# Scratch transposes issued from GpSimd's queue instead of SyncE's, with shorter pauses, in a two-layer decoder trunk

## The chip, the cores and the metric

The kernel runs on one core of a Trainium2 chip. The metric is the device time of one execution in microseconds. A core has five engines that run side by side, each working through its own queue of instructions in order: TensorE (PE; PEld is its weight load), VectorE (DVE), ScalarE (ACT), GpSimd (POOL) and SyncE (SP). They meet at semaphores. Transfers are begun by an instruction in one engine's queue and are then carried by 16 DMA engines.

## The reference, cut to what matters

Two layers over 256 positions of width 2048, each a token mixer and a dense SwiGLU FFN (hidden width 5632). Layer 0 mixes with stick-breaking attention, layer 1 with a gated DeltaNet.

```python
def swiglu(h, w_gu, w_down):
    gate, up = jnp.split(h @ w_gu, 2, axis=-1)
    return (jax.nn.silu(gate) * up) @ w_down

for i in range(DEPTH):
    h = rms_norm(x, mix_norm[i])
    y = stick_breaking_mixer(...) if i == 0 else gated_deltanet_mixer(...)
    x = x + y
    x = x + swiglu(rms_norm(x, ffn_norm[i]), ffn_w_gu[i], ffn_w_down[i])
```

In the attention mixer q and k are normed per head and then multiplied, `z = q k^T`, so both are needed with the head's 128 columns on the partitions. The FFN's product `silu(gate) * up` is needed with its hidden columns on the partitions for the product with `w_down`. Both come out of TensorE the other way round, with the positions on the partitions. They have to be transposed.

## The kernel before

**Products.** All weights are streamed from HBM in pieces (a unit: two tiles of 128 rows by 512 columns, 512 KB). Each operand, weight or activation, is split into a high part in the fast format and a low part with the rest, and three products (high-high, high-low, low-high) give the float32 result. ScalarE makes the high part of a weight piece (`convert`, by `act`, line 328), VectorE the low part (`tt`, line 332), and TensorE multiplies (`mm`, line 354). A stretch of both FFNs runs six pairs of blocks by a scheme with seven products in place of eight (`seven`); its sums of weights are more work for VectorE. Two or three pieces are converted ahead of TensorE.

**Transposes through scratch.** In 36 places a transpose is done without TensorE: VectorE transposes 32 x 32 squares in place (`nc.vector.transpose`, lines 897 and 939), four transfers write the rows to a DRAM scratch tile (`way`), and two transfers read it back in another order. Here this is called a turn, its transfers the writes and the reads. A write moves 32 partitions of 32 x 32 floats in pieces of 128 bytes (128 KB), a read 128 partitions of 4 x 128 floats in pieces of 512 bytes (256 KB). `turn` (from line 891) does it for q and k of the four head groups (8 turns) and for parts of the input of three norms (`TURNED`, 6 turns). `turned_pairs` (from line 933) does it for the FFN's 22 hidden blocks, and then splits the result into high (`kh`) and low (`kl`) parts by `operands_of`. For q a scaling by `qgain` on ScalarE follows, for k nothing: TensorE reads it as it is. At the norms ScalarE and VectorE make `hTh` and `hTl` from it.

**Queues.** All transfers, weights (`load`, line 519) and turns (`dma`, line 367), are begun by SyncE. A read waits for the writes of its turn.

**What sets the order.** The program is written out while a planner keeps a clock for each engine (`self.t`). Work around the products is in tasks, generators that yield where they would wait. At each small step of the products `tick` resumes those tasks whose planned time (`task.ready`) has come, and what a task then issues goes into the engines' queues at that place. So the planned durations decide where in ScalarE's and VectorE's queues the split stands, between the weight conversions. A wrong one does no harm to the result, since semaphores hold the real order, but an instruction that stands too early holds up the queue behind it. For a transfer begun by SyncE the planner counts 0.46 of SyncE's clock, 1.55 to begin, the bytes at a rate, and 0.55 to land. `WAY` is a pause between the transposes and the first write in `turned_pairs` (`TURN` in `turn`), `NAP` the one between its transfers (`STEP` in `turn`): they keep SyncE's queue free for weight loads between the writes.

Of the kernel before, what the change touches and what calls it, by code (L numbers as in the profile page):

```python
# [15 lines left out]
P = 128  # L16
D = 2048
S = 256
NT = S // P
# [12 lines left out]
class Slots:  # L32
# [37 lines left out]
    def put(self, *items):  # L70
        self.free.extend(items)
# [86 lines left out]
class Trunk:  # L158
# [20 lines left out]
    CONST = 14.0  # L179
    EARLY = 6  # L180
    LATER = 1.5
    WAY, NAP = 3.0, 1.2
    TURN, STEP = 1.0, 1.2
    TURNED = ((1, 0), (1, 1), (2, 0), (2, 1), (3, 0), (3, 1))
    GDN_ORDER = [('qk', 0), ('ba',), ('v', 0), ('qk', 1), ('z', 0), ('v', 2), ('v', 1), ('z', 1), ('qk', 2), ('qk', 3), ('v', 3), ('z', 2), ('z', 3), ('out', 0, 4), ('out', 4, 8), ('qk', 4), ('v', 4), ('qk', 5), ('v', 5), ('z', 5), ('z', 4), ('qk', 7), ('v', 6), ('qk', 6), ('out', 8, 16), ('v', 7), ('z', 6), ('z', 7), ('out', 16, 24), ('out', 24, 32)]

# [179 lines left out]
    def dma(self, out, in_):  # L366
        self.nc.sync.dma_start(out, in_)
        n = 4
        for d in out.shape:
            n *= d  # L370
        self.cur.ends("dma", self.transfer(n * (2 if out.shape[-1] * 4 <= 512 else 1), self.cur.begins("dma")))

    def transfer(self, nbytes, ready):
        issue = max(self.t["sp"], ready, self.t["pe"])
        self.t["sp"] = issue + 0.46
        self.t["dma"] = max(self.t["dma"], issue + 1.55) + nbytes / 3.6e5
        return self.t["dma"] + 0.55
# [513 lines left out]
    def turn(self, parts, back=False, src=None):  # L891

        way = yield from self.ways.get()
        for i, s in enumerate(parts):
            self.nc.vector.transpose(s, src[i] if src else s)
            self.spend("dve", 0.07 + 0.00104 * NB)
            self.weave()
        self.cur.later = self.TURN  # L900
        yield
        flat = way[:]
        both = parts[0].tensor is parts[1].tensor and parts[1].offset - parts[0].offset == NB
        apart = not back and not both

        rows = (flat.rearrange("(c t) j -> c (t j)", t=2) if apart else flat).rearrange("(b i) j -> i b j", i=32)
        k = 0
        for a in range(4):
            m = slice(32 * a, 32 * a + 32)
            for n in range(1 if both else 2):  # L910
                if both:
                    dst, at = rows[:, :, m], self.joined(parts[0], 2)[m, :]
                elif back:
                    dst, at = rows[:, 16 * n:16 * n + 16, m], parts[n][m, :]
                else:
                    dst, at = rows[:, :, n * P + 32 * a:n * P + 32 * a + 32], parts[n][m, :]
                self.dma(dst, at.rearrange("p (b j) -> p b j", j=32))
                k += 1
            self.cur.nap = self.STEP if a < 3 else None
            yield  # L920
        for n in range(2):
            if back:
                self.dma(parts[n].rearrange("p (k c) -> p k c", k=4), flat.rearrange("(k t p) c -> t p k c", t=NT, p=P)[n])
            elif apart:
                self.dma(parts[n].rearrange("p (k c) -> p k c", k=2),
                         flat.rearrange("(c t) j -> c (t j)", t=2)[S * n:S * n + S, :].rearrange("(k p) c -> p k c", p=P))
            else:
                self.dma(self.joined(parts[0], 2).rearrange("p (k s) -> p k s", k=4)[:, :, n * P:(n + 1) * P],
                         flat[n * NB:(n + 1) * NB, :].rearrange("(k p) s -> p k s", p=P))
        yield  # L930
        self.ways.put(way)

    def turned_pairs(self, tok, stage, ops, put):

        way = yield from self.ways.get()
        for s, t in zip(self.cut(stage, NB), self.cut(tok, NB)):
            self.nc.vector.transpose(s, t)  # L939
            self.spend("dve", 0.07 + 0.00104 * NB)  # L940
            self.weave()
        self.cur.later = self.WAY
        yield

        rows = way[:].rearrange("(b i) j -> i b j", i=32)
        for a in range(4):
            m = slice(32 * a, 32 * a + 32)
            self.dma(rows[:, :, m], stage[m, :].rearrange("p (b j) -> p b j", j=32))
            self.cur.nap = self.NAP if a < 3 else None
            yield  # L950
        for t in range(NT):
            self.dma(tok.rearrange("p (k s) -> p k s", k=4)[:, :, t * P:(t + 1) * P],
                     way[t * NB:(t + 1) * NB, :].rearrange("(k p) s -> p k s", p=P))
            self.cur.nap = self.NAP if t < NT - 1 else None
            yield
        self.ways.put(way)
        if stage is not tok:
            self.duos.put(stage)
        for n, l in enumerate(self.cut(tok, NB)):
            pair = yield from self.pairs.get()  # L960
            self.operands_of(ops[2 * n:2 * n + 2], pair, l.rearrange("p (k s) -> p k s", k=2))
        put()


    def ffn_units(self, layer, norm, nxt, last, before, ahead=0):
# [52 lines left out]
        for b, n in zip(mids, turn):  # L1018
            b.sets = (n,)
# [773 lines left out]
```

## Time and profile before

| | before |
|---|---|
| time, median of 3 runs | 2709.56 us (2708.41 to 2709.73) |
| profiled execution | 2705.98 us |
| its span on the core | 2704.3 us |
| granted TensorE clock | 1.00 |
| mean DMA rate over the span | 198 GB/s |

The page lists the busy time of each engine, the chain of work that ended last, the waits and the transfers. In a row of the waits, the instruction that waited stands left of the arrow and what it waited for right of it, then the total in us, the number of times and the longest. In a row of the timeline the first two numbers are the start (us from the span's start) and the duration; brackets hold the idle time before it and what ended that. In the view by stretches, the columns after the two lengths are the busy time (with the number of instructions) of PE, PEld, DVE, ACT and POOL, then the granted clock, the DMA engines' busy share and GB/s. In the table of a tile, a row of transfers has the shortest, median and longest time that the begin took in its queue (ns), then the first and last start.

### The profile page before, as it was taken

To read this page: it belongs to the slowest core of one execution; us is meant where nothing else is said; L and a number is where in the kernel's file an instruction comes from. 1 tells how busy PE (TensorE), PEld (TensorE's weight loads), DVE (VectorE), ACT (ScalarE), POOL (GpSimd) and SP (SyncE) were. 2 spreads that over 40 slices of the span, in tenths; PEclk is the share of its full clock that TensorE was granted. 3 is DMA by queue.
4 is the path that set the end of the run, shared out by engine and by line. 5 is a ranking of instruction groups with operands and counts; after the bars stand their busy time and mean duration, and the time that the engine had idled before them with its cause. 6 is when DMAs were issued, how large, how long until landed. Compare 5 with 4: busy or idle time off the path is not lost.

```text
span 2704.3 us, 39527 instructions
## 1 busy us (share of the span) xinstructions
PE 2669.4 (99%) x14730; PEld 2274.6 (84%) x14730; DVE 2182.7 (81%) x3451; ACT 1491.8 (55%) x1961; POOL 11.2 (0%) x95
## 2 busy tenths in 40 slices
PE   9999999999999999999999999999999999999999
PEld 7888888888888888888888888888878888888887
DVE  6556568899999897678778887887679899989885
ACT  6555556554555554565665556645575555555453
POOL 0000000000000000000000000000000000000000
PEclk9999999999999999999999999999999999999999
DMA  7766775787676777855656556556567767767776
GB/s 245 202 185 196 219 211 164 208 231 212 203 218 205 208 211 233 227 174 172 182 143 195 159 161 175 168 153 186 170 191 212 223 196 220 217 188 218 226 209 188
DMA packets 487611, 534.41 MB, mean 198 GB/s; under 512 B 188087, under 2 KB 267258, under 8 KB 487418
## 3 DMA queue, kind: packets, MB, share of 16 engines
q1 hardware_dynamic: 487370, 531.87, 67.1%
q8 instruction: 115, 1.88, 0.3%
q14 instruction: 78, 0.64, 0.1%
q10 hardware_dynamic: 48, 0.02, 0.0%
HBM read 508.20 MB, written 23.59 MB: 197 GB/s over the span
## 4 chain that ended last, share of the span: by engine, by line
PE 83%; DVE 10%; issue 2%; ACT 2%; DMA 2%; SPq 0%; ACTq 0%; DVEq 0%
PE acc L354 61%; PE bank L354 20%; DVE w L332 5%; DVE slabs L332 2%; PE bank L363 1%; DMA slab<-in_ffn_w_gu_dram 1%; ACT slabs L328 1%; ACT w L328 1%; DVE slab L338 1%; DVE slab L332 1%; DVE slab L939 1%; DMA slab<-in_ffn_w_down_dram 0%; ACT slab L328 0%; DVE x L332 0%; DMA w<-in_ffn_w_gu_dram 0%
## 5 line engine op out<-in xcount | busy, mean ns | idle before, releaser
L332 DVE TENSOR_TENSOR w<-w,w 128x1024 fp32r<-128x1024 f32 (+2 forms) x746 | 946.3, 1285 | 249.0 <-ACT w L328 247.6
L328 ACT ACTIVATE w<-w 128x1024 fp32r<-128x1024 f32 (+2 forms) x650 | 802.8, 1244 | 417.8 <-PE acc L354 347.0
L354 PE MATMUL acc<-w,hTh 128*128 128x512 f32 (+1 forms) x3232 | 925.0, 369 | 9.1 <-DVE w L332 8.4
L354 PEld LDWEIGHTS acc<-w,hTh 128*128 128x128 f32 x3232 | 585.9, 189 | 120.5 <-DVE w L332 14.5
L354 PE MATMUL acc<-w,hTl 128*128 128x512 f32 (+1 forms) x1616 | 590.2, 365 | 3.1 <-DVE hTl L338 3.1
L328 ACT ACTIVATE slabs<-slab 128x1024 fp32r<-128x1024 f32 x264 | 279.3, 1058 | 431.9 <-DMA slab<-in_ffn_w_gu_dram 123.8
L332 DVE TENSOR_TENSOR slabs<-slab,slabs 128x1024 fp32r<-128x1024 f32 x264 | 321.5, 1218 | 93.1 <-ACT slabs L328 93.1
L354 PE MATMUL acc<-w,kh 128*128 128x512 f32 x1184 | 369.6, 393 | 0.0
L354 PEld LDWEIGHTS acc<-w,hTl 128*128 128x128 f32 x1616 | 304.5, 188 | 53.5 <-DVE hTl L338 3.9
L332 DVE TENSOR_TENSOR w<-w 128x256 f32<-128x256 f32 (+1 forms) x576 | 291.2, 508 | 9.8 <-DMA w<-in_ffn_w_gu_dram 2.6
L354 PEld LDWEIGHTS acc<-w,kh 128*128 128x128 f32 x1184 | 218.8, 188 | 43.7
L354 PE MATMUL acc<-w,kl 128*128 128x512 f32 x592 | 230.7, 390 | 0.0
L354 PE MATMUL acc<-slabs,hTh 128*128 128x512 f32 x608 | 190.1, 392 | 2.8 <-DVE slabs L332 2.8
L354 PE MATMUL bank<-w,wide 128*128 128x256 f32 x1296 | 178.9, 283 | 0.0
L354 PEld LDWEIGHTS bank<-w,wide 128*128 128x128 f32 x1296 | 165.8, 192 | 0.0
L354 PE MATMUL bank<-slabs,hTh 128*128 128x512 f32 x512 | 159.9, 392 | 3.1 <-DVE slabs L332 3.1
L354 PE MATMUL bank<-slabs,kh 128*128 128x512 f32 x512 | 159.6, 392 | 3.4 <-DVE slabs L332 3.4
L354 PE MATMUL acc<-slabs,kh 128*128 128x512 f32 x480 | 149.9, 392 | 2.1 <-DVE slabs L332 1.9
L354 PEld LDWEIGHTS acc<-slabs,hTh 128*128 128x128 f32 x608 | 111.0, 188 | 25.1 <-DVE slabs L332 4.9
L354 PEld LDWEIGHTS acc<-w,kl 128*128 128x128 f32 x592 | 111.1, 188 | 23.4
L354 PE MATMUL acc<-slabs,hTl 128*128 128x512 f32 x304 | 118.3, 389 | 0.0
L328 ACT ACTIVATE slab<-bank 32x128 f32<-32x128 f32 (+4 forms) x181 | 67.9, 379 | 89.3 <-PE bank L354 87.1
(216 smaller groups left out, 2933.4 us busy)
## 6 DMA issues: line engine op xcount, KB each, us to landing
w<-in_ffn_w_gu_dram SPq DMA_DIRECT2D x212, 512.0 KB, 4.5
slab<-in_ffn_w_gu_dram SPq DMA_DIRECT2D x140, 512.0 KB, 4.5
w<-in_gdn_w_in_dram SPq DMA_DIRECT2D x129, 512.0 KB, 4.3
slab<-in_ffn_w_down_dram SPq DMA_DIRECT2D x124, 512.0 KB, 4.5
w<-in_sb_w_in_dram SPq DMA_DIRECT2D x96, 512.0 KB, 4.5
w<-in_gdn_w_in_dram SPq DMA_DIRECT2D x128, 256.0 KB, 3.7
w<-in_gdn_w_out_dram SPq DMA_DIRECT2D x64, 512.0 KB, 4.4
w<-in_ffn_w_down_dram SPq DMA_DIRECT2D x52, 512.0 KB, 5.5
```

What stands on the lines that cost most here:

```text
L328: self.nc.scalar.activation(out, in_, func, **kw)
L332: self.nc.vector.tensor_tensor(out, a, b, op=op)
L338: self.nc.vector.scalar_tensor_tensor(out, a, s, b, op0=op0, op1=op1)
L354: self.nc.tensor.matmul(out, lhsT, rhs, start=start, stop=stop, skip_group_check=True)
L363: self.nc.tensor.transpose(out, in_, self.ident[:p, :p])
L939: self.nc.vector.transpose(s, t)
```

## The change

A new method `way_dma` begins a transfer in GpSimd's queue (`nc.gpsimd.dma_start`), and the writes and reads of both `turn` and `turned_pairs` use it. For the planner such a transfer no longer takes time of SyncE or of the DMA's clock: it is planned to have landed 4.0 us (`OWN`) after it is begun. The pauses become shorter: `WAY` 3.0 to 0.5, `NAP` 1.2 to 0.5, `TURN` 1.0 to 0.3, `STEP` 1.2 to 0.5.

```diff
-    WAY, NAP = 3.0, 1.2
-    TURN, STEP = 1.0, 1.2
+    WAY, NAP = 0.5, 0.5
+    TURN, STEP = 0.3, 0.5
+    OWN = 4.0
...
+    def way_dma(self, out, in_):
+
+        self.nc.gpsimd.dma_start(out, in_)
+        self.cur.ends("dma", max(self.cur.begins("dma"), self.t["pe"]) + self.OWN)
...
@@ turn
-                self.dma(dst, at.rearrange("p (b j) -> p b j", j=32))
+                self.way_dma(dst, at.rearrange("p (b j) -> p b j", j=32))
...
-                self.dma(parts[n].rearrange("p (k c) -> p k c", k=4), flat.rearrange("(k t p) c -> t p k c", t=NT, p=P)[n])
+                self.way_dma(parts[n].rearrange("p (k c) -> p k c", k=4), flat.rearrange("(k t p) c -> t p k c", t=NT, p=P)[n])
...
-                self.dma(parts[n].rearrange("p (k c) -> p k c", k=2),
+                self.way_dma(parts[n].rearrange("p (k c) -> p k c", k=2),
...
-                self.dma(self.joined(parts[0], 2).rearrange("p (k s) -> p k s", k=4)[:, :, n * P:(n + 1) * P],
+                self.way_dma(self.joined(parts[0], 2).rearrange("p (k s) -> p k s", k=4)[:, :, n * P:(n + 1) * P],
...
@@ turned_pairs
-            self.dma(rows[:, :, m], stage[m, :].rearrange("p (b j) -> p b j", j=32))
+            self.way_dma(rows[:, :, m], stage[m, :].rearrange("p (b j) -> p b j", j=32))
...
-            self.dma(tok.rearrange("p (k s) -> p k s", k=4)[:, :, t * P:(t + 1) * P],
+            self.way_dma(tok.rearrange("p (k s) -> p k s", k=4)[:, :, t * P:(t + 1) * P],
```

The order that comes of it differs on every engine. SyncE's queue before, at one turn of the first FFN, has its four writes and two reads among the loads of weights (names with `in_ffn`):

```order
L367 DMA way_117<-slab 32x32x32
L519 DMA slab<-in_ffn_w_gu_dram 128x2x512
L367 DMA way_117<-slab 32x32x32 x2
L519 DMA w_2928<-in_ffn_w_gu_dram 128x2x512
L367 DMA way_117<-slab 32x32x32
L519 DMA slab<-in_ffn_w_gu_dram 128x2x512
L519 DMA w_122<-in_ffn_w_gu_dram 128x2x512
L519 DMA slab<-in_ffn_w_gu_dram 128x2x512
L367 DMA slab<-way_117 128x4x128
```

Now SyncE has loads alone at that place, and the turns stand one behind the other in GpSimd's queue, with the semaphores for which they wait (DMASW: a transfer begun by GpSimd):

```order
L376 DMA way_117<-slab 32x32x32 [waits DMASW5_49,DMASW6_49,DMASW4_49,DVE_49]
L376 DMA way_117<-slab 32x32x32 [waits DMASW7_49]
L376 DMA way_117<-slab 32x32x32 x2
L376 DMA slab<-way_117 128x4x128 [waits DMASW6_49,DMASW1_49,DMASW7_49,DMASW0_49,PE_49]
L376 DMA slab<-way_117 128x4x128 [waits PE_49]
L376 DMA way_118<-slab 32x32x32 [waits DVE_49]
L376 DMA way_118<-slab 32x32x32 x3
```

The writes wait for VectorE's transposes, the first read for the turn's four writes. The next turn's writes stand behind these reads.

ScalarE's queue at the split of the same turn, before (the names with 128x1024 and 128x1792 are conversions of weights, kh the high part of the turned operand):

```order
L328 ACTIVATE slabs<-slab 128x1024 x2
L328 ACTIVATE w_123<-w_2928 128x1792
L328 ACTIVATE slabs<-slab 128x1024
L328 ACTIVATE w_123<-w_122 128x1792
L328 ACTIVATE slabs<-slab 128x1024
L328 ACTIVATE w_123<-w_122 128x1792
L328 ACTIVATE slabs<-slab 128x1024
L328 ACTIVATE w_123<-w_2928 128x1792
L328 ACTIVATE slabs<-slab 128x1024
L328 ACTIVATE kh_81<-slab 128x512
L328 ACTIVATE kh_83<-slab 128x512
L328 ACTIVATE w_123<-w_122 128x1792
```

and now, from the same conversions on:

```order
L329 ACTIVATE slabs<-slab 128x1024 x2
L329 ACTIVATE w_123<-w_2928 128x1792
L329 ACTIVATE slabs<-slab 128x1024
L329 ACTIVATE w_123<-w_122 128x1792
L329 ACTIVATE kh_81<-slab 128x512
L329 ACTIVATE kh_83<-slab 128x512
L329 ACTIVATE slabs<-slab 128x1024
L329 ACTIVATE w_123<-w_122 128x1792
L329 ACTIVATE slabs<-slab 128x1024
L329 ACTIVATE w_123<-w_2928 128x1792
```

The two kh stand five conversions earlier. The transposes on VectorE, the start of the turn, stand where they stood.

TensorE's queue at the first use of a turned k, before: products with weights, then those of q and k, which begin with a mask (negmask):

```order
L354 MATMUL acc_106<-w_123,hTh_65 128x512 x2
L354 MATMUL acc_106<-w_123,hTl_66 128x512
L354 MATMUL acc_107<-w_123,hTh_65 128x512 x2
L354 MATMUL acc_107<-w_123,hTl_66 128x512
L354 MATMUL acc_106<-w_123,hTh_65 128x512 x2
L354 MATMUL acc_106<-w_123,hTl_66 128x512
...
L354 MATMUL acc_106<-w_123,hTh_67 128x512 x2
L354 MATMUL acc_106<-w_123,hTl_68 128x512
L354 MATMUL bank_109<-negmask,identr 128x384
L354 MATMUL bank_109<-slab 128x256
```

and now:

```order
L355 MATMUL acc_106<-w_123,hTh_65 128x512 x2
L355 MATMUL acc_106<-w_123,hTl_66 128x512
L355 MATMUL bank_109<-negmask,identr 128x384
L355 MATMUL bank_109<-slab 128x256
L355 MATMUL bank_109<-slab 128x128
L355 MATMUL bank_110<-negmask,identr 128x384
```

The products of q and k have moved ahead of 18 products with weights.

## The prediction

> **What bounds the kernel now.** I read the page first, then its waits by engine, then single turns in the timeline. A turn is one transpose through DRAM scratch: four writes (way<-slab) and two reads (slab<-way).
>
> ```profile
> span 2704.3 us, 39527 instructions
> PE 2669.4 (99%) x14730; PEld 2274.6 (84%) x14730; DVE 2182.7 (81%) x3451; ACT 1491.8 (55%) x1961; POOL 11.2 (0%) x95
> PE 83%; DVE 10%; issue 2%; ACT 2%; DMA 2%; SPq 0%; ACTq 0%; DVEq 0%
> ```
>
> TensorE is busy 2669.4 of 2704.3 us. The change leaves its work alone, so nothing can be won but the 34.9 us in which it stands idle. GpSimd (POOL) works 11.2 us in all; its queue is free. The view by stretches says where the idle time lies (second column: PE busy):
>
> ```profile
> 100.00:200.00 100.00, 99.80 (x457) 83.08 (x456) 60.05 (x72) 54.26 (x75) 0.00 (x0) 1.00 0.67 192
> 600.00:700.00 100.00, 97.14 (x582) 86.27 (x581) 92.17 (x118) 51.02 (x43) 0.00 (x0) 1.00 0.68 202
> 1400.00:1500.00 100.00, 100.00 (x528) 82.06 (x527) 85.71 (x181) 57.97 (x82) 1.00 (x10) 1.00 0.62 184
> ```
>
> The attention and DeltaNet stretches lose next to nothing; the two FFNs lose 1 to 4 us in each 100, and there VectorE (fourth column) is busy over 90%. TensorE's own waits, longest first:
>
> ```profile
> PE acc L354 <- DVE w L332: 8.4, 16, 1.0
> PE bank L354 <- DVE slabs L332: 6.5, 5, 1.6
> PE acc L354 <- DVE slabs L332: 4.7, 9, 0.9
> PE bank L363 <- DMA slab<-in_mix_norm_dram: 4.7, 1, 4.7
> PE acc L354 <- DVE hTl L338: 3.1, 2, 1.5
> ```
>
> Apart from the start (4.7), TensorE waits only for VectorE, which makes the low halves of weights and operands: 22.7 us in these four rows. No wait of TensorE names a turn. A turn shows on ScalarE alone:
>
> ```profile
> L367 SPq DMA_DIRECT2D way<-slab x144: 459/476/3367, 46.8 to 2642.4; - x144
> L367 SPq DMA_DIRECT2D slab<-way x72: 366/458/2547, 57.5 to 2648.6; - x72
>   ACT kh L328: 25.2, 14
> DMA to landing us min/median/max: 3.6/5.2/7.1
> ```
>
> 144 writes and 72 reads are 36 turns: 22 in the FFNs, 8 for q and k, 6 at the norms. ScalarE waited for 14 of the FFN's operands, 25.2 us together, and TensorE lost nothing by it.
>
> **The change, part by part.** *SyncE loses 216 begins.* Each cost 0.46 us of its queue, and sometimes much more:
>
> ```profile
> 655.84 0.46 SPq L367 DMA_DIRECT2D way<-slab  x1
> 657.15 0.48 SPq L519 DMA_DIRECT2D slab<-in_ffn_w_gu_dram  x1
> 657.69 3.06 SPq L367 DMA_DIRECT2D way<-slab  x2
> 660.85 1.63 SPq L519 DMA_DIRECT2D w<-in_ffn_w_gu_dram  x1
> ```
>
> Two writes held SyncE for 3.06 us with a weight load behind them. That goes. But the loads run ahead of TensorE, whose waits name VectorE, so the most that it frees is a part of those 22.7 us. I count 8: the 3.1 for hTl, which follow a turned norm, and a quarter of the other 19.6. If turns come late, this gain is spent in their waits, and then I count none.
>
> *GpSimd gains 216 begins.* No DMA is begun by GpSimd in this trace, so the price has to be bounded. Call it w for a write and r for a read. Lower end: SyncE's median, 0.46 for either. Upper end: SyncE's longest, 3.37 and 2.55. A write is 1024 pieces of 128 B, a read 512 of 512 B, and if GpSimd lays them out one by one, pieces count; so I set r to w/2 between the ends. Where SyncE was held, two writes took 3.06, some 1.5 each. I see no ground for GpSimd, all of whose other work are short fills, to be quicker than that, and take w = 2.0, r = 1.0, about the middle of the ends. Below nothing it cannot be: every begin is an instruction of its queue.
>
> *How long a turn then takes.* GpSimd has nothing else in its queue there, so it begins the four writes as soon as VectorE has transposed, whatever the pauses say; the first read waits in its queue until the writes have landed. From transposes to data it is 4w + 2r and twice the way from a begin's end to landing. On a queue without weights ahead I take the shortest landing, 3.6 less the begin's 0.46 = 3.1. So **H = 4w + 2r + 6.3**, here 8 + 2 + 6.3 = 16.3 us. With SyncE's price it would be 9.0 at the shortest and, with the median 5.2 in place of 3.6, 12.2.
>
> *How much time the new order leaves it.* This is what the shorter pauses do: the splits (kh on ScalarE, kl on VectorE) are written earlier in their engines' queues, and a queue waits in order. One turn of the first FFN:
>
> ```profile
> 648.40 1.29 DVE L939 STREAM_TRANSPOSE slab<-slab 128x512 f32<-128x512 f32 x2
> 661.78 1.69 ACT L328 ACTIVATE w<-w 128x1792 fp32r<-128x1792 f32 x1
> 675.83 1.15 ACT L328 ACTIVATE kh<-slab 128x512 fp32r<-128x512 f32 x2 [1.73 <-DMA slab<-way]
> 676.89 1.69 ACT L328 ACTIVATE w<-w 128x1792 fp32r<-128x1792 f32 x1
> 678.61 2.09 DVE L332 TENSOR_TENSOR w<-w,w 128x768 fp32r<-128x768 f32 x2 [0.82 <-ACT w L328]
> 683.31 0.40 PE L354 MATMUL acc<-w,hTh 128*128 128x256 f32 x2
> ```
>
> Before, the transposes end at 649.69 and kh starts at 675.83: 26.1 us. In the new order kh stands five weight conversions earlier, right behind the one that ends at 661.78 + 1.69 = 663.47: 13.8 us are left. I did the same for all 22 FFN turns: two (one in each layer, whose split stands far back in both orders) keep their time, the other 20 move by three to six conversions and are left 9.6 to 13.8, mean **11.9 us**. The shortest, transposes to the end of the conversion ahead of kh, 918.15 to 927.78:
>
> ```profile
> 917.45 0.70 DVE L939 STREAM_TRANSPOSE slab<-slab 128x512 f32<-128x512 f32 x1
> 926.72 1.06 ACT L328 ACTIVATE slabs<-slab 128x1024 fp32r<-128x1024 f32 x1 [1.04 <-PE bank L354]
> ```
>
> Behind kh stands the next weight conversion, on which TensorE depends: its low half ended at 678.61 + 2.09 = 680.70 and TensorE wanted it at 683.31, a slack of 2.6 us. For the other turns it is 0.7 to 3.4, mostly; I take 2.0. So an FFN turn costs TensorE H - 13.9: 2.4 us, times 20 = **48**.
>
> The q scaling moves up by two conversions:
>
> ```profile
> 43.95 1.30 DVE L897 STREAM_TRANSPOSE slab<-slab 128x512 f32<-128x512 f32 x2
> 52.99 1.06 ACT L328 ACTIVATE w<-w 128x1024 fp32r<-128x1024 f32 x1 [1.66 <-PE acc L354]
> 62.18 1.34 ACT L328 ACTIVATE slab<-slab,qgain 128x512 f32<-128x512 f32 x2 [0.28 <-DMA slab<-way]
> 65.64 1.30 DVE L897 STREAM_TRANSPOSE slab<-slab 128x512 f32<-128x512 f32 x2
> 84.76 0.34 PE L354 MATMUL bank<-negmask,identr 128*128 128x384 f32 x1
> ```
>
> It stands behind the conversion that ends at 54.05, 8.8 us after the transposes (45.25). Over the four q turns this is 9.5 on average, and about as much at the six norm turns. VectorE has more room there (60% busy in the stretch 100:200), so I give them more slack, 3.4 (an estimate): H - 12.9 = 3.4 us, times 10 = **34**.
>
> The four k turns have no slack, since TensorE itself reads k. Its products with k stood at 84.76 and now stand 18 matmuls earlier. At 0.22 us each (457 of them in the stretch 100:200) that is 80.8, 13.9 after the transposes end at 66.94: H - 13.9 = 2.4, times 4 = **10**.
>
> Sum: 48 + 34 + 10 = 92. The profiled execution took 2705.98 us (1.7 beyond its span), so 2798 for such a one; the median of the runs shown, 2709.56, lies 3.6 above it and would become 2802. I say **2800 us**.
>
> At the upper end (3.37, 2.55, landings at 5.2) H is 28.0: 20 x 14.1 + 10 x 15.1 + 4 x 14.1 = 489, or 3200 us. At the lower end H is at most 12.2, and all three terms are nothing.
>
> The Trainium skill (page "DMA: Bandwidth & Descriptors", section "Anatomy of one DMA — SWDGE (gpsimd) path") counts a DMA of GpSimd's at about 2.0 us plus its bytes at 436 GB/s, with the making of descriptors "small, variable". By that a write would take 2.3 us and a read 2.6, and a turn, by an estimate from this page, some 5 to 7 us: no wait at all, the first rival below. The same page ("Issuing engine by pattern") names the sync queue for simple loads and stores and calls it generally faster than GpSimd's. Neither can be seen in a trace that has no DMA of GpSimd's.
>
> **Rivals.** *Faster:* GpSimd begins a write in under 1.3 us. Then H = 5w + 6.3 stays below 12.8, each split finds its data or costs no more than its slack, and SyncE's relief is all that shows: 2709.6 - 8 = 2702 us. For it: ScalarE's present waits of up to 5 us cost TensorE nothing. Against it: 1024 pieces in 1.3 us, when SyncE, held, needed 1.5. The point that decides is w = 1.3.
>
> *No change:* w about 1.3 to 1.5, where small losses eat the relief, or a relief of nothing because TensorE's waits come from a VectorE that is 92% busy: 2709 us.
>
> *Far slower:* w over 2.6. Then H is over 19.3, the three terms are 108 + 64 + 22 = 194 and more: 2904 to 3200. GpSimd's queue would then also be long, and where two turns follow each other closely the second waits for the first.
>
> That the transfers don't move is excluded: in the new program all 216 stand in GpSimd's queue. Nor do they meet its fills, since no turn lies between the first and last DeltaNet group.
>
> **How the numbers follow.** Forecast (w 1.5 to 2.6; 2715 to 2904 by itself) 0.36; far slower 0.21; faster 0.26; no change 0.17. A difference of 0.2%, 5.4 us, is about the least that can be told from none here. So slower 0.57, within 0.2% 0.17, faster 0.26. The range reaches from 2697 (all of the relief and a little more) to 2960 (w near 2.9); about 0.15 lies above and 0.05 below.
>
> **What would show it.** Right: GpSimd's begins of writes near 2 us in the table of the tile way, ScalarE's wait for slab<-way risen from 25 us to over 100, TensorE's idle time from 35 to over 100, in waits for VectorE right behind a kh. Wrong: begins under 1.3 us, or waits on kh that stay below 2 us each; or long waits on kh with TensorE still at 2669 of 2704, in which case the slack was larger than I read.

## The result, and the profile after

| | before | changed |
|---|---|---|
| median of 4 runs | 2709.09 us (2708.41 to 2709.73) | 2737.36 us (2733.21 to 2742.68) |
| ratio to before, 95% interval | | 1.0105 (1.0088 to 1.0123) |
| profiled execution: its time, its span | 2705.98 us, 2704.3 us | 2733.21 us, 2731.5 us |

The change costs 28 us. 2800 had been forecast, 91 us more than before: the sign is right, the size three times too large. The changed kernel's page, its span and the busy time of the engines:

```profile
span 2731.5 us, 39750 instructions
PE 2677.9 (98%) x14730; PEld 2279.2 (83%) x14730; DVE 2179.7 (80%) x3451; ACT 1487.5 (54%) x1961; POOL 178.7 (7%) x311
```

TensorE (PE) is idle for 53.6 us of the span where it was 34.9, and its busy time rose by 8.5 us with the same 14730 matmuls. GpSimd (POOL) works 178.7 us in place of 11.2. The table of the scratch tile `way` in the changed kernel, with begins (min, median and max in ns), who waited (us in total, times) and landing:

```profile
L376 POOL DMA_DIRECT2D way<-slab x144: 784/788/932, 45.6 to 2660.6; - x144
L376 POOL DMA_DIRECT2D slab<-way x72: 752/764/779, 54.9 to 2669.2; - x72
  ACT kh L329: 66.6, 20
  ACT slab L329: 23.3, 4
  ACT hTh L329: 23.1, 6
  PE bank L355: 13.6, 3
DMA to landing us min/median/max: 2.9/5.1/8.4
```

A write's begin takes 0.79 us and a read's 0.76, not 2.0 and 1.0. ScalarE's waits did rise, from 25.2 to 66.6 us at kh alone, and for the first time TensorE itself waits for a turn (`PE bank`). TensorE's own waits, longest first (total, times, longest):

```profile
PE bank L355 <- DMA slab<-way: 13.6, 3, 5.0
PE bank L355 <- DVE slabs L333: 11.1, 9, 1.6
PE acc L355 <- DVE w L333: 7.2, 18, 1.3
PE bank L364 <- DMA slab<-in_mix_norm_dram: 4.8, 1, 4.8
PE bank L355 <- issue: 4.5, 1, 4.5
```

The new rows are the first and the last: four waits of 4 to 5 us, 18.2 us together (one lies where the trace names no releaser, and it stands in front of the same products). They are the four products of attention that read k. Two of the stretches shown for before, in the changed kernel (second column PE busy, after the engines PEclk, the granted TensorE clock):

```profile
100.00:200.00 100.00, 96.02 (x433) 80.50 (x432) 53.48 (x64) 51.55 (x72) 9.30 (x12) 0.97 0.60 180
600.00:700.00 100.00, 98.69 (x590) 87.56 (x590) 92.69 (x118) 52.35 (x44) 4.65 (x6) 1.00 0.67 208
```

Attention, which had 457 matmuls in its stretch of 100 us, has 433, and the clock is 0.97 where it was 1.00. The FFN's stretch lost nothing: 590 matmuls beside 582. So the time went in attention, where the forecast had put 24 of its 92 us (k, and q's part of the second term), and not in the FFNs.

How the first of the four waits comes about can be read from three engines. The changed kernel's timeline of ScalarE:

```profile
53.06 1.06 ACT L329 ACTIVATE w<-w 128x1024 fp32r<-128x1024 f32 x1 [1.66 <-PE acc L355]
60.95 1.34 ACT L329 ACTIVATE slab<-slab,qgain 128x512 f32<-128x512 f32 x2 [6.82 <-DMA slab<-way]
62.19 1.04 ACT L329 ACTIVATE w<-w 128x1024 fp32r<-128x1024 f32 x1
63.14 1.24 ACT L329 ACTIVATE slab<-acc,rstd 128x512 f32<-128x512 f32 x2
```

that of VectorE,

```profile
63.26 1.23 DVE L333 TENSOR_TENSOR w<-w,w 128x1024 fp32r<-128x1024 f32 x1 [7.88 <-ACT w L329]
70.27 1.30 DVE L903 STREAM_TRANSPOSE slab<-slab 128x512 f32<-128x512 f32 x2
```

and that of TensorE:

```profile
81.89 0.34 PE L355 MATMUL bank<-negmask,identr 128*128 128x384 f32 x1
86.77 1.46 PE L355 MATMUL bank<-slab 128*128 128x256 f32 x4 [4.54 <-issue]
```

ScalarE waits 6.82 us for q. Behind q in its queue stand the squares for the norm of k (`slab<-acc,rstd`), which VectorE needs before it can norm and transpose k. So k's transposes end at 71.57; before, they ended at 66.94 (the prediction's row at 65.64). TensorE has its weights converted ahead and does not slow down in the meantime. It comes to the products of q and k 10.3 us behind the end of the transposes, and k's data come 15 to 16 us behind it.

Behind each of these waits the granted clock is a half for some us. The stretches of the changed kernel at and behind the first:

```profile
87.20:90.60 3.40, 3.40 (x12) 2.80 (x11) 0.56 (x1) 2.25 (x5) 0.00 (x0) 0.50 0.02 5
90.60:100.00 9.40, 9.40 (x49) 8.10 (x48) 5.34 (x8) 7.84 (x16) 0.00 (x0) 1.00 0.18 48
```

The four half-clock times are 3.4, 6.8, 3.4 and 3.4 us, 17.0 together, so by an estimate about 8.5 us of work are lost in them. 18.2 + 8.5 = 26.7 us, nearly the whole loss.

### The profile page after: what moved, and what is told of

It is laid out like the page before. It is cut to its first block, busy times and chain, and to the rows that moved or that the text cites. A ratio compares the mean times of both kernels' runs of the same rounds, so it can differ in the third digit from the quotient of the medians.

```text
span 2731.5 us, 39750 instructions
## 1 busy us (share of the span) xinstructions
PE 2677.9 (98%) x14730; PEld 2279.2 (83%) x14730; DVE 2179.7 (80%) x3451; ACT 1487.5 (54%) x1961; POOL 178.7 (7%) x311
## 4 chain that ended last, share of the span: by engine, by line
PE 70%; DVE 8%; DMA 2%; issue 2%; ACT 1%; POOL 0%; DVEq 0%; ACTq 0%; POOLq 0%
PE acc L355 48%; PE bank L355 21%; DVE w L333 4%; DVE slabs L333 2%; PE bank L364 1%; DMA slab<-way 1%; DMA way<-slab 1%; DVE slab L339 1%; DVE slab L333 1%; DVE slab L945 1%; DVE x L333 1%; DMA slab<-in_ffn_w_down_dram 0%; POOL way L376 0%; ACT w L329 0%; ACT slabs L329 0%
## 5 line engine op out<-in xcount | busy, mean ns | idle before, releaser
L376 POOL DMA_DIRECT2D way<-slab x144 | 113.1, 792 | 1556.0 <-DVE slab L945 849.3
L355 PEld LDWEIGHTS acc<-w,kl 128*128 128x128 f32 x592 | 111.2, 188 | 23.6
```

What stands on the lines that cost most here:

```text
L355: self.nc.tensor.matmul(out, lhsT, rhs, start=start, stop=stop, skip_group_check=True)
L376: self.nc.gpsimd.dma_start(out, in_)
```

## The experiments

Theory A is the reading above: TensorE itself waits for k, and the half clock adds to it. Theory B is the prediction's: splits of the FFN hold ScalarE up longer than the weights behind them can bear. Theories C to H come with the runs that test them.

Each time stands beside runs of the kernel before on the same chip (2709.25 to 2709.69 us). One table for all. "Idle" is TensorE's pauses of over 0.1 us summed from the trace, in attention (20 to 400 us) and in the two FFNs (400 to 1110 and from 1960 us); "half" is the time at half clock before TensorE's last product; "kh" is ScalarE's waits at the FFN splits for `slab<-way`. These four columns are of one profiled execution each, the time is the median of several.

| kernel | us | ratio to before | idle attention | idle FFNs | half | kh |
|---|---|---|---|---|---|---|
| before | 2709.09 | | 0.6 | 23.4 | 0 | 25.2 |
| changed | 2737.36 | 1.0105 (1.0088 to 1.0123) | 19.1 | 23.6 | 17.0 | 66.6 |
| q, k, norms on SyncE, old pauses | 2716.12 | 1.0024 (1.0015 to 1.0034) | 0.6 | 30.4 | 3.4 | 73.2 |
| FFN turns on SyncE, old pauses | 2736.07 | 1.0098 (1.0081 to 1.0114) | 20.2 | 21.5 | 23.8 | 30.0 |
| TensorE kept busy at k | 2731.63 | 1.0083 (1.0065 to 1.0100) | 1.4 | 23.0 | 0 | 69.5 |
| k's users later | 2713.58 | 1.0013 (1.0004 to 1.0023) | 3.8 | 25.5 | 3.4 | 71.1 |
| q's scaling later | 2717.20 | 1.0029 (1.0020 to 1.0038) | 4.7 | 24.4 | 6.8 | 71.0 |
| k later, FFN data 1.5 us later | 2725.59 | 1.0060 (1.0047 to 1.0072) | 2.3 | 32.9 | 13.6 | 93.2 |
| k later, FFN data 3.0 us later | 2755.46 | 1.0164 (1.0147 to 1.0181) | 3.2 | 46.2 | 37.4 | 126.8 |
| GpSimd, old pauses | 2709.48 | 0.9998 (0.9989 to 1.0007) | 3.9 | 21.9 | 3.4 | 7.4 |
| SyncE, short pauses | 2721.25 | 1.0042 (1.0027 to 1.0057) | 4.0 | 28.7 | 6.8 | 27.1 |
| changed order, begun by SyncE | 2823.65 | 1.0420 (1.0406 to 1.0435) | 19.9 | 69.9 | 71.4 | 148.8 |
| planner told 6.5 us | 2702.12 | 0.9974 (0.9963 to 0.9985) | 0.6 | 19.2 | 0 | 3.6 |
| the same again | 2702.08 | 0.9972 (0.9961 to 0.9984) | 0.6 | 20.0 | 0 | 1.4 |
| that order, begun by SyncE | 2723.21 | 1.0051 (1.0037 to 1.0064) | 0.6 | 36.3 | 10.2 | 63.3 |
| planner told 8.0 us | 2715.60 | 1.0020 (1.0011 to 1.0029) | 0.0 | 30.9 | 0 | 0 |

### Which turns cost: q, k and the norms put back

```diff
@@ turn
-                self.way_dma(dst, at.rearrange("p (b j) -> p b j", j=32))
+                self.dma(dst, at.rearrange("p (b j) -> p b j", j=32))
...
-    TURN, STEP = 0.3, 0.5
+    TURN, STEP = 1.0, 1.2
```

> The 14 turns of q, k and the norms go back to SyncE with their old pauses; the 22 FFN turns stay on GpSimd with short ones. Theory A (TensorE itself waits for the turned k, 18 us in four places, and runs at half clock for a while behind each): these waits go, the first 400 us are as before, and the time is 2703 to 2712 us. Theory B (the splits stand too early in ScalarE's queue and hold up the weight conversions, FFN turns above all, as the prediction had it): the FFN's share stays, 2725 us or more.

2716.12 us. The four waits at k are gone (idle in attention 0.6 us), and with them 21 of the 28 us. 6.5 us remain, more than I had allowed the FFN turns: idle time in the FFNs is 7 us above the kernel before.

### The mirror: FFN turns put back

```diff
@@ turned_pairs
-            self.way_dma(rows[:, :, m], stage[m, :].rearrange("p (b j) -> p b j", j=32))
+            self.dma(rows[:, :, m], stage[m, :].rearrange("p (b j) -> p b j", j=32))
...
-    WAY, NAP = 0.5, 0.5
+    WAY, NAP = 3.0, 1.2
```

> The mirror image: FFN turns back on SyncE with old pauses, the turns of q, k and the norms on GpSimd with short ones. Theory A: the loss stays whole, 2730 to 2742 us, four waits of TensorE for slab<-way of 4 to 5 us each. Theory B: most of the loss goes, 2715 us or less.

2736.07 us, as slow as the whole change, with four waits of 4.39 to 5.19 us at k and 23.8 us at half clock. The loss sits in the q and k turns; the FFN turns, on which the prediction had put the largest term, are 1 to 2 us of it by this run and 6.5 by the one before. The two halves don't add up exactly (6.5 + 26.5 against 28.3), and why is not shown: in the run before this one the splits stand in the same rows of ScalarE's queue as in the changed kernel.

### TensorE kept busy in front of k

```diff
@@ sb_attend, before the first product with k
+            for _ in range(32 if pr == 0 and h == 0 else 0):
+                self.nc.tensor.matmul(z[:, :W], self.identr, self.negmask, start=True, stop=False, skip_group_check=True)
             self.mm(z[:, :W], self.identr, self.negmask, start=True, stop=False)
```

> The changed kernel with 32 more mask products (negmask, written again into the same bank, 0.16 us each) ahead of the first use of each k, so that TensorE is busy for some 5 us while it would wait. If idle TensorE is what brings the half clock behind each k, the clock stays at 1.0 and about 8 us are won: 2727 to 2730 us for one like the changed kernel's 2737. If the half clock has another cause (or costs nothing), the time is the changed kernel's or up to 3 us above it, since the filler may outlast the wait.

2731.63 us, a little above the expected 2727 to 2730. The repeated matmuls fill the waits without bringing k any sooner. No time at half clock is left, and the time falls by 5.7 us. The halved clock is thus a part of the loss that can be taken away by itself. The 5.7 us are a rough figure (the intervals of the two kernels overlap) and rather too small: the first 32 fills take 5.6 us where TensorE had waited 4.5, so they outlast the wait.

### k's users put later

```diff
@@ sb_proj
+        if what == "k":
+            self.cur.nap = 5.3
+            yield
         st[what] = toks
```

> The changed kernel, with one more pause of 5.3 us of the planner's time behind the turn of k, so that the products of q and k stand two units of weights later in TensorE's queue. Nothing else is changed by hand. Theory A: the four waits and the half clock behind them go, 2703 to 2712 us. Theory B: within 5 us of the changed kernel, 2730 us or more.

2713.58 us, just above the expected 2703 to 2712: 23.8 of the 28.3 us are back though q still waits (24.5 us in the table of `way`). The products with k now stand behind 349 matmuls of TensorE's queue in place of 328.

### q's scaling put later, k left where it is

```diff
@@ sb_proj
         if what == "q":
+            self.cur.nap = 5.3
+            yield
             for s in toks:
                 self.act(s, s, scale=self.qgain)
```

> The changed kernel with one edit: a pause of 5.3 us behind each q turn, which puts the scaling of q back to the row of ScalarE's queue where it stood before the change (row 42; changed kernel: 38). k's users stay 18 matmuls earlier than before. Theory F (ScalarE's wait at q, 5.8 us on average, makes k's transposes 4.6 us late, and this is what TensorE meets at k): the four gaps of 4 to 5 us shrink to 2 or less, since k's data then come 16 us behind transposes that end 4.6 us sooner; little half clock; 2711 to 2722 us. Theory G (k's own place, 18 matmuls too early, makes the gap): gaps of 4 to 5 us as before, 2733 to 2741.

2717.20 us: 20.2 us are back, and k's users stand behind 328 matmuls as in the changed kernel. All rows of TensorE and VectorE stand in the changed kernel's order; ScalarE's alone differ. ScalarE's timeline in this kernel:

```profile
57.73 1.37 ACT L329 ACTIVATE slab<-acc,rstd 128x512 f32<-128x512 f32 x2 [0.98 <-PE acc L355]
61.90 1.34 ACT L329 ACTIVATE slab<-slab,qgain 128x512 f32<-128x512 f32 x2
```

that of VectorE at k's transposes, and of TensorE at the same products as above:

```profile
65.36 1.30 DVE L903 STREAM_TRANSPOSE slab<-slab 128x512 f32<-128x512 f32 x2
```

```profile
82.05 0.49 PE L355 MATMUL bank<-slab 128*128 128x128 f32 x2 [0.62 <-DMA slab<-way]
```

The squares for k start at 57.73, not 63.14; the transposes end at 66.66, not 71.57; TensorE waits 0.62 us, not 4.54 (0.6, 0.9 and 1.8 us at the other three k). What TensorE met at k was ScalarE's wait at q, handed on by two engines. Either edit alone removes most of it, which is why neither a place nor a wait by itself is "the" cause: k is too early only because it is also late.

### How much a split may wait: FFN data 3.0 and 1.5 us later

On the kernel with k's users later:

```diff
@@ turned_pairs, between the two reads
+            for _ in range(24 if t == 0 else 0):
+                self.nc.gpsimd.memset(self.held, 0.0)
```

> The kernel with k's users later (2713.6 us), and in each FFN turn GpSimd fills a small unused tile 24 times (0.16 us each, 3.9 us) between its two reads, so that the data come 3.9 us later and no order changes. Theory A (the splits have far more slack than the 2.0 us of the prediction): ScalarE's waits grow by some 20 x 3.9 = 78 us, TensorE's gaps in the FFN by under 10, and the time is 2714 to 2724. Theory B (slack of 2.0 us, and already used up): 20 x 3.9 = 78 us more, 2790.

A fill took 0.124 us and not 0.16, so the delay was 24 x 0.124 = 3.0 us. The time rose by 41.9 us. Both theories are off: there is more room than 2.0 us, or the waits of the changed kernel would have cost TensorE already, but it ends soon. With 12 fills:

> The kernel with k's users later (2713.6 us) with 12 fills of a small unused tile (0.124 us each as the earlier run showed, 1.5 us) between the two reads of each FFN turn; with 24 (3.0 us) it took 41.9 us more. Theory H (a split has room up to a wait of about 5 us, and only what goes beyond reaches TensorE; now they wait 3.3 on average): 5 to 15 us more, 2718 to 2729. If the cost is linear from zero (no room at all): 21 more, 2734.

12.0 us more, as theory H has it. The rows of the splits, from the tables of `way` of the run with 12 and then of that with 24 fills:

```profile
  ACT kh L330: 93.2, 20
```

```profile
  ACT kh L330: 126.8, 20
```

Per wait that is 3.3 us in the changed kernel (idle time in the FFNs as before), 3.6 with k's users later, 4.7 with 1.5 us of delay (12.0 us lost by 20 splits, 0.6 each) and 6.3 with 3.0 (41.9 us, 2.1 each, about 0.9 of it by the half clock). Single waits of the changed kernel say the same. Seventeen of its 20 waits are under 5 us, and TensorE is idle for no more than 0.03 us in the 14 us behind any of them. Three are longer (5.9 to 6.5 us), with 1.0 to 1.9 us of idle time behind each. ScalarE's row of one and TensorE's row behind it:

```profile
583.39 1.15 ACT L329 ACTIVATE kh<-slab 128x512 fp32r<-128x512 f32 x2 [6.44 <-DMA slab<-way]
```

```profile
587.14 0.50 PE L355 MATMUL bank<-slabs,hTh 128*128 128x512 f32 x1 [1.05 <-DVE slabs L333]
```

So the room is about 5 us at most splits of this order. It is less at some: with 24 fills, waits of 3.3 to 4.7 us have 0.2 to 0.6 us of idle TensorE behind them, and in the run with q, k and the norms on SyncE two waits of 3.4 and 4.0 us have 1.1 to 1.2.

### Is it the queue or the order? GpSimd with the old pauses

```diff
-    WAY, NAP = 0.5, 0.5
-    TURN, STEP = 0.3, 0.5
+    WAY, NAP = 3.0, 1.2
+    TURN, STEP = 1.0, 1.2
```

> GpSimd's queue alone: the turns are begun by GpSimd, the pauses are the old ones (3.0, 1.2, 1.0, 1.2). The data come by the same 14 to 17 us, but the readers stand late, as before. Theory A: 2705 to 2713, no gap over 2 us at the k turns. Theory C (the queue itself costs): 2720 or more. If SyncE's relief of 8 us that the fast rival counted on is there, it shows here as 2701 to 2704, since nothing else differs.

2709.48 us, the kernel before to 0.1%. On balance GpSimd's queue costs nothing, and a relief of SyncE does not show here. The order is not quite that of before, though: q's scaling stands three rows earlier in ScalarE's queue, and TensorE is idle for 3.9 us in attention (0.6 before) and 21.9 in the FFNs (23.4 before). A small loss and a small relief may cancel; this run can't part them.

### The short pauses alone, on SyncE

```diff
@@ the kernel before
-    WAY, NAP = 3.0, 1.2
-    TURN, STEP = 1.0, 1.2
+    WAY, NAP = 0.5, 0.5
+    TURN, STEP = 0.3, 0.5
```

> The short pauses alone: the turns stay on SyncE. The planner models SyncE's landings itself, and puts the products with k behind 358 matmuls (before: 346), so TensorE should not wait for k. Theory A: 2705 to 2715 us. A theory by which short pauses are the fault, on whatever queue: 2725 or more.

2721.25 us, between the two. TensorE waits at most 2.4 us for k, but is idle for 28.7 us in the FFNs (23.4 before).

### The changed order, begun by SyncE

```diff
@@ way_dma
-        self.nc.gpsimd.dma_start(out, in_)
+        self.nc.sync.dma_start(out, in_)
```

> The changed kernel's order of work to the last row, with the turns begun by SyncE. From transposes to data SyncE's turns take about 4 x 0.48 + 2 x 0.46 + 2 x (5.2 - 0.5) = 12.3 us where no weight load stands ahead, GpSimd's 14 to 17; TensorE comes for k 13.9 us behind the transposes. Theory A (the loss is TensorE's own wait for k): the four gaps shrink below 1.5 us each, no or little half clock, 2704 to 2716. If the new order costs by itself, whatever the queue: 2730 or more.

2823.65 us: my expectation, 2704 to 2716, is 108 us off. With every row on TensorE, ScalarE and VectorE in the same order, SyncE costs 86 us more than GpSimd. The table of `way` in this kernel:

```profile
L376 SPq DMA_DIRECT2D way<-slab x144: 450/556/5303, 47.8 to 2748.5; - x144
  ACT kh L329: 148.8, 20
  ACT hTh L329: 29.6, 6
DMA to landing us min/median/max: 2.7/4.8/8.1
```

The begins are shorter (0.56 us beside 0.79) and they land no later, yet kh waits 148.8 us. SyncE's timeline at the first k turn shows why:

```profile
72.75 0.37 SPq L525 DMA_DIRECT2D w<-in_sb_w_in_dram  x1
73.17 1.06 SPq L376 DMA_DIRECT2D way<-slab  x2
74.33 3.10 SPq L525 DMA_DIRECT2D w<-in_sb_w_in_dram  x1
77.48 1.06 SPq L376 DMA_DIRECT2D way<-slab  x2
78.65 3.32 SPq L525 DMA_DIRECT2D w<-in_sb_w_in_dram  x2
82.82 0.92 SPq L376 DMA_DIRECT2D slab<-way  x2
```

Weight loads stand between a turn's transfers and hold the queue 3.1 us (one load) and 3.3 us (two). From the end of the transposes to the end of the last read's begin a turn took 14.6 us on average here (11.5 to 20.3), in the changed kernel 10.7 (9.3 to 13.3), in the kernel before 18.4. I had worked SyncE's turn out from its median begins with no load ahead, which a turn among weight loads does not get.

### The planner told a longer time

```diff
-    OWN = 4.0
+    OWN = 6.5
```

> All turns stay on GpSimd's queue with the short pauses; only the planner is told that such a transfer's data come 6.5 us after its begin in place of 4.0. The products with k then stand behind 346 matmuls again, as before the change (the changed kernel: 328). Theory A (the loss is TensorE's own wait at the four k turns and the half clock behind it): the four gaps of 4 to 5 us go, no half clock, 2706 to 2715 us. Theory C (the queue itself costs, wherever the work stands): still 2725 or more. Theory B (the splits of the FFN lie behind the loss): they move back too, so B allows 2709 as well; this run tells A from C alone.

2702.12 us, 7.2 us faster than the kernel before and faster than theory A allowed. The planner now puts k's users behind 346 matmuls and q's scaling back to its row of before. The splits go back by only two to four rows of ScalarE's queue, of the three to eight by which the change had moved them, and that is enough to end nearly all of their waits. The page's row of TensorE and, from the table of `way`, the only row of an engine other than GpSimd that waits for a turn:

```profile
PE 2668.8 (99%) x14730; PEld 2274.9 (84%) x14730; DVE 2182.5 (81%) x3451; ACT 1491.4 (55%) x1961; POOL 178.7 (7%) x311
```

```profile
  ACT kh L329: 3.6, 4
```

Once more, beside the next two runs:

> The kernel with 6.5 us once more, beside the other three on the same chip: 2700 to 2705 if its gain of 7 us on the kernel before holds; within 3 us of the kernel before if it was the chip's.

2702.08 us, ratio 0.9972 (0.9961 to 0.9984). It beats both kernels.

### The same order, begun by SyncE

The edit to `way_dma` shown above, on the kernel with 6.5.

> The kernel told of 6.5 us (2702.1 us), with nothing changed but the engine that begins the turns: SyncE in place of GpSimd. The order of work on TensorE, ScalarE and VectorE is the same to the last row. Theory D (the 7 us that it wins on the kernel before come from where its readers stand, no wait left at the splits): 2700 to 2704 here too. Theory E (they come from SyncE, which no longer holds weight loads behind writes; the relief of 8 us of the prediction's fast rival): 2707 to 2712 here.

2723.21 us, slower than either theory allowed, and 21 us slower than with GpSimd. Theory D, by which the order alone wins, falls; E has the sign, and too small a size. Its table of `way`:

```profile
  ACT kh L329: 63.3, 20
```

The splits wait 63.3 us where they waited 3.6 and 1.4. ScalarE also waits longer for the FFNs' weights. Its row in the run begun by GpSimd, then in this one:

```profile
ACT slabs L329 <- DMA slab<-in_ffn_w_gu_dram: 98.4, 50, 5.8
```

```profile
ACT slabs L329 <- DMA slab<-in_ffn_w_gu_dram: 134.4, 58, 5.6
```

No wait at a split is over 5.0 us here, so late weights may carry a part of the 21 us beside late turns; the runs don't part the two. Either way the gain needs both: transfers on a queue without weight loads, and readers that stand where the data come.

### 8.0 us

```diff
-    OWN = 4.0
+    OWN = 8.0
```

> The planner is told 8.0 us in place of 6.5: products with k behind 355 matmuls, splits a little later again. If the gain of the run with 6.5 is what waits are left out (3.6 us of ScalarE's waits remain there), nothing more is to be had: 2700 to 2706. If readers that stand too late begin to cost, 2708 or more.

2715.60 us. No wait at the splits or at k is left, and it is slower than with 6.5 all the same. Its waits of TensorE:

```profile
PE acc L355 <- DVE w L333: 14.1, 24, 1.3
...
PE acc L355 <- ACT hTh L329: 3.4, 2, 1.7
```

TensorE waits 14.1 us for low halves of weights (7.7 with 6.5), and 3.4 us for the operand of a norm that is now made too late. Readers can also be too late.

## Why the prediction was right in sign and wrong in size

- **H, 16.3 us from transposes to data: nearly right, by two errors that cancel.** Measured it is 15.5 on average (13.9 to 17.5). The begins are 4 x 0.79 + 2 x 0.76 = 4.7 us where I had 10, since pieces of 128 bytes don't slow GpSimd: a write of 1024 pieces and a read of 512 take nearly the same. But the two landings and the gap ahead of the first begin are 10.8 where I had 6.3: I took the shortest landing of the kernel before, 3.6, for a queue without weights ahead, and the median there is 5.1. The Trainium skill (page "DMA: Bandwidth & Descriptors", section "Anatomy of one DMA — SWDGE (gpsimd) path") has the making of descriptors small, and there the trace agrees (0.79 us). By an estimate from its fit a write would take 2.3 us, and here the trace disagrees: 5.1 at the median of all 216 transfers, beside the weight loads.
- **The FFN term, 20 x 2.4 = 48: the step that failed.** The waits came nearly as forecast: H - 11.9 was 4.4, is 3.6 by the measured H, and 3.3 in the trace. What failed is the slack of 2.0 us, by which even the measured H would cost 20 x 1.6 = 32 us; the room is about 5 at most splits. I had taken the slack of one conversion behind kh. But ScalarE is busy only 54% of the time, and right behind the split of the prediction's own rows the kernel before has a pause, in ScalarE's timeline:

```profile
678.48 1.04 ACT L328 ACTIVATE slabs<-slab 128x1024 fp32r<-128x1024 f32 x1
683.51 1.06 ACT L328 ACTIVATE slabs<-slab 128x1024 fp32r<-128x1024 f32 x1 [3.98 <-PE acc L354]
```

  That ScalarE makes up for the wait in such pauses is my reading of these rows; the size of the room is what the runs show. Idle time in the FFNs is 23.6 us after and 23.4 before.
- **The q and norm term, 10 x 3.4 = 34: wrong in kind for q, nothing for the norms.** q waits 5.8 us on average, about what H - 9.5 gives. I priced it as time that TensorE loses at the next weights. It loses none there, at q or at the norms: of the 19.1 us that it is idle in attention, 18.2 are the four waits for k, and its idle time in the FFNs is that of before. q's wait goes to k's transposes instead, and the run with q's scaling put back shows that it carries 20 of the 28 us.
- **The k term, 4 x 2.4 = 10: the right place, under-sized to 27.** I gave k 13.9 us, counted from transposes that end where they ended before. They end 4.6 us later (in the first group), so that the waits are 4.5 us each, 18.2 in all, and the half clock adds about 8.5.
- **The relief of SyncE, 8 us in the fast rival.** A gain of that size shows where the readers don't wait: 7.2 and 7.6 us with 6.5, none with the old pauses. That SyncE's relief alone gives it is not shown, since the order differs from that of before in both. Its deciding point, w under 1.3, was passed with 0.79, and the kernel was slower all the same, because the landings made good what the begins saved. A point set on one summand of H could not decide.

## What to carry to other kernels

Moving transfers to another queue and telling the planner how long they take are two changes: the first was worth 86 us at one order of work and 21 at another, and the second, set 2.5 us lower than the best of the three values tried, turned a gain of 7 into a loss of 28. Before pricing a wait by the engine it stands on, look at what is queued behind it and follow that to the next transfer. A wait that an engine absorbs can still start the next turn late. Room behind a wait is more than the next instruction's slack (by my reading, all that the engine has idle behind it), and it has an end: the first 1.5 us of delay cost 12, the next 1.5 cost 30.

## What the runs showed of the hardware

- GpSimd begins a transfer in 0.75 to 0.93 us, whatever its pieces (1024 of 128 bytes or 512 of 512). SyncE takes 0.39 to 0.56 at the median and up to 5.3 us.
- TensorE's clock is halved for 3.4 or 6.8 us around waits of 4 to 5 us, and around smaller ones: with 3.0 us of delay the half clock came nine times in the two FFNs at pauses of 2.5 us at the longest, while the waits of 1.57 us in the kernel before brought none. The Trainium skill (page "TensorE: Matmul & The Clock Gate", section "HAM oscillation — how this bites in real kernels") gives the rule that no pause should exceed about 3.4 us. In this run shorter ones do it too: single pauses of 1.9 to 2.5 us, or several that come to 1.6 to 2.8 us within 6.8. They don't do it always: a single pause of 2.22 us in the same run brought none, and one stretch of 3.4 us at half clock (from 1575.6) stands behind no pause. TensorE's rows behind the longest of these pauses and behind the pause of 2.22 us, then the stretches from there:

```profile
578.95 0.80 PE L356 MATMUL acc<-slabs,kh 128*128 128x512 f32 x1 [2.47 <-ACT slabs L330]
2313.23 0.50 PE L356 MATMUL bank<-slabs,kh 128*128 128x512 f32 x1 [2.22 <-DVE slabs L334]
```

```profile
578.95:585.75 6.80, 6.34 (x16) 4.78 (x17) 6.73 (x9) 5.61 (x6) 0.00 (x0) 0.50 0.53 152
2313.30:2320.00 6.70, 6.70 (x40) 5.95 (x41) 6.67 (x8) 3.50 (x3) 2.59 (x4) 1.00 0.86 245
```
